# Decay factors from spread rows and a minimum, and local scores whose low key part meets half the rows

## The chip, the cores and the metric

The kernel runs on one core of a Trainium2 chip. The metric is the device time of one execution in microseconds (us). Before the change three runs gave 1501.08, 1501.22 and 1502.55 us; their median is 1501.22 us.

## The reference

The kernel computes one layer of an encoder trunk over 1024 tokens of width 1024: a mixer that joins windowed attention with a gated delta rule run in both directions, then a cross-attention into 256 memory tokens, then a SwiGLU FFN. The change touches two places in the mixer. In the windowed attention, 8 query heads of width 64 share 2 key heads, and a block of 128 queries sees itself and its two neighbour blocks:

```python
kw, vw = band(k), band(v)
scores = jnp.einsum('bnqhgd,bnkhd->bnhgqk', qb, kw) * (ATTN_HEAD_DIM ** -0.5)
```

In the delta rule, each chunk has a triangular matrix of decays, the exponent of a difference of running sums of g:

```python
g = jnp.cumsum(g.reshape(b, h, n, c), axis=-1)
decay = jnp.exp(jnp.where(incl, g[..., :, None] - g[..., None, :], -jnp.inf))
```

The rule runs once forward and once on the flipped sequence, with a g of its own for each direction.

## The kernel before

The mixer works in chunks of 128 tokens, so there are 8 chunks (`NT`). The product of a weight column block with all tokens (`proj`, L279) is 48 matmuls on TensorE of 512 columns each, because each operand is split in a rounded high part and a low rest (`split`, L100) and three of the four part products are kept.

A list written by hand, `ORDER_1` (L37), names the steps of the first stage: the projections `q`, `k`, `v` of four heads with a short convolution (`conv`, L291), and between them `E` (`decays`), `K` (`turned_keys`), `U` (`key_products`), `C` (`query_products`) and `B` (`base_inverse`). A scheduler then lays each engine's instructions in an order of its own from that program, so a step can stand far from where the list has it; every engine and each DMA queue runs its list in order. Nearly all DMAs are on SyncE's queue (SP).

`decays(h)` (L479) makes the two tiles `E` for head h, each of 4 chunks. Forward and backward decays stand in one tile, on the two sides of the diagonal. Four matmuls (two directions, and the high and the low part of g) of a triangular 0/1 matrix (`mL_r`, `mU_r`) with `gm`, the g of a chunk spread over the other triangular matrix, add up in one PSUM bank; `E` is the exponent of that. VectorE makes `gm` for heads 0 and 1 (L488), ScalarE for heads 2 and 3 (L491). `E` multiplies the key products `U` (L513) and the query products `pc` (L521).

The PSUM tiles of this stage come from a pool of five banks (`small`, L204). The tile that the change adds for the spread rows is taken from pool `ra`, whose two buffers of tag `rr` the attention projections use later.

`window(n, g)` (L663) does the local attention of query block n and key head g, 16 times. The keys `khi`, `klo` hold the 64 key channels twice, in rows 0 to 63 and in rows 64 to 127. `qs` holds the rounded queries in rows 0 to 63 and their low rest in rows 64 to 127 (a ScalarE cast at L676, then GpSimd on the lower half at L677); one matmul with `khi` over 128 rows so adds high times high and low times high. For each of four heads there are two matmuls, with `khi` and with `klo` (L685), of 384 columns, or 256 at the ends of the sequence; VectorE takes the scores out of PSUM with the band and the row's maximum (L687). The scores' banks come from pool `pw` with two buffers, shared with the transposes `ptw` of the weights. The windows run in between the projections of the second stage (`ORDER_2`) and the scan of the delta rule (`scan`, L830, matmuls L844) and the memory projections (`pck`, L984).

Of the kernel before, what the change touches and what calls it, by code (L numbers as in the profile page):

```python
# [19 lines left out]
P = 128  # L20
# [3 lines left out]
NT = S // P  # L24
HALF = 512
# [51 lines left out]
def tile_hybrid_block(  # L77
# [6 lines left out]
    nc = tc.nc  # L84
# [57 lines left out]
    mU_r = sm.tile([P, P], F32R, name="mU_r")  # L142
    mL_r = sm.tile([P, P], F32R, name="mL_r")
# [44 lines left out]

    d_beta = [dram.tile([32, P], F32, name=f"d_beta{g}") for g in range(2)]
# [14 lines left out]
    def small():  # L204
        return ps.tile([P, 512], F32, tag="ps", name="ps")
# [54 lines left out]
    with tc.issue_after(scaled.ins):  # L260
        nc.vector.tensor_copy(mU_r, cm["mU"])
        nc.vector.tensor_copy(mL_r, cm["mL"])

# [109 lines left out]
    ghi = sm.tile([P, 2, 4, NT], F32, name="ghi")  # L373
    glo = sm.tile([P, 2, 4, NT], F32, name="glo")
    ghr = t1.tile([P, 2, 4, NT], F32R, tag="ghr", name="ghr")
    nc.vector.tensor_copy(ghr, G)
    nc.vector.tensor_copy(ghi, f32(ghr))
    nc.vector.tensor_tensor(glo, G, ghi, ALU.subtract)

# [99 lines left out]
    def decays(h):  # L479

        for b in range(2):
            pa = small()
            n = 0
            for d, (mi, ml) in enumerate((("mUi", mL_r), ("mLi", mU_r))):
                for part in (ghi, glo):
                    gm = t2.tile([P, 4, P], F32R, tag="gm", name="gm")
                    if h < 2:
                        nc.vector.tensor_tensor(gm, bc(part[:, d, h, 4 * b:4 * b + 4], 2, (P, 4, P)), bc(cm[mi], 1, (P, 4, P)),  # L488
                                                ALU.mult)
                    for j in range(4 if h > 1 else 0):  # L490
                        nc.scalar.activation(gm[:, j, :], cm[mi], AF.Identity, scale=part[:, d, h, 4 * b + j:4 * b + j + 1])  # L491
                    nc.tensor.matmul(pa, ml, gm.rearrange("p c n -> p (c n)"), start=(n == 0), stop=(n == 3))
# [170 lines left out]
    def window(n, g):  # L663
# [13 lines left out]
        nc.gpsimd.tensor_tensor(qs[64:128], qr[64:128], f32(qs[64:128]), ALU.subtract)  # L677

# [3 lines left out]
        for hh in range(4):  # L682
            pp = pw.tile([P, 512], F32, tag="pw", name="psw")
            for i, kk in enumerate((khi, klo)):
                nc.tensor.matmul(pp[:, 0:w], qs[:, hh, :], kk, start=(i == 0), stop=(i == 1))  # L685
# [1209 lines left out]
```

## Time and profile before

| what | value |
|---|---|
| median of three runs | 1501.22 us |
| span of the profiled execution | 1497.9 us |
| time around the span, against the median | 3.3 us |
| mean granted TensorE clock | 0.995 |
| busy PE, weight load, VectorE, ScalarE, GpSimd | 98%, 83%, 74%, 52%, 25% of the span |
| DMA | 256.35 MB, 171 GB/s mean |

The profiled execution shows its span, from the first to the last instruction; its own time with what lies around the span is not listed beside it, so the three runs give it: about 3.3 us more than the span. A matmul's time in the trace runs from its start to a modelled end, and matmuls overlap in the array, so PE looks busy nearly always; how fast PE works is read from the distance between two starts. PEld is the load of the stationary operand, and a form such as 32*128 beside an operation gives the rows and columns of the array that it uses.

### The profile page before, as it was taken

The page shows a single profiled execution, that of the slowest core. Times are in us where ns is not written, and L with a number is a line of the kernel's source. Part 1 is how long each engine was busy: PE and PEld are TensorE (multiplying, and loading weights), DVE is VectorE, ACT ScalarE, POOL GpSimd, SP SyncE. Part 2 cuts the span into 40 slices and gives each one's busy share as a digit, 9 for nine tenths or more (in the row PEclk, how much of TensorE's full clock was granted, in tenths as well). Part 3 has the DMA queues.
Part 4 walks back from the last instruction along what each step waited for, and adds up shares of the span by engine and source line. Part 5 has one row for each costly group of instructions (what it writes and reads, how often), then busy time and mean ns, then how long its engine had stood idle before and what let it go on. Part 6 is the DMA issues. An engine that isn't in the chain of part 4 may idle for free.

```text
span 1497.9 us, 21340 instructions
## 1 busy us (share of the span) xinstructions
PE 1467.6 (98%) x7437; PEld 1239.1 (83%) x7437; DVE 1108.8 (74%) x1804; ACT 776.3 (52%) x1600; POOL 374.3 (25%) x411
## 2 busy tenths in 40 slices
PE   7999999999999999999999999999999999999998
PEld 6888878888999878888888877888888888888787
DVE  5878998577897866538767887686867774795666
ACT  7678844568567664555554774323223232544533
POOL 0011232442246213342201002343433342000030
PEclk9999999999999999999999999999999999999999
DMA  6244554657996585444855553343533433953355
GB/s 205 71 120 137 142 168 135 168 173 222 297 305 211 158 310 204 163 146 157 277 174 194 183 197 119 121 141 105 168 123 113 138 109 103 351 183 99 105 181 170
DMA packets 254169, 256.35 MB, mean 171 GB/s; under 512 B 18129, under 2 KB 186222, under 8 KB 254062
## 3 DMA queue, kind: packets, MB, share of 16 engines
q1 hardware_dynamic: 252141, 250.80, 52.7%
q0 software_dynamic: 768, 2.10, 0.5%
q10 hardware_dynamic: 1152, 2.10, 0.4%
q8 instruction: 58, 0.95, 0.3%
q14 instruction: 50, 0.40, 0.1%
HBM read 178.63 MB, written 73.70 MB: 168 GB/s over the span
## 4 chain that ended last, share of the span: by engine, by line
PE 73%; DVE 9%; ACT 4%; issue 2%; DMA 2%; SPq 1%; POOL 0%; DVEq 0%; ACTq 0%
PE pE L1511 8%; PE pD L1511 8%; PE pA L1511 6%; PE pmg L1105 6%; PE pcq L276 6%; PE pdX L1733 6%; PE pst L1324 5%; PE pdA L1733 4%; PE pB L1511 4%; PE pg L276 3%; PE psc L844 3%; PE pdD L1733 2%; PE pdX L1842 2%; PE pcs L1195 2%; PE pco L1222 1%
## 5 line engine op out<-in xcount | busy, mean ns | idle before, releaser
L103 ACT CAST whi<-wraw 128x1024 fp32r<-128x1024 f32 x96 | 100.7, 1050 | 119.5 <-DMA wraw<-in_w_gate_up_dram 40.0
L276 PE MATMUL pg<-hlo,whi 128*128 128x512 f32 x352 | 140.5, 399 | 0.0
L276 PE MATMUL pg<-hhi,whi 128*128 128x512 f32 x352 | 139.6, 396 | 0.0
L276 PE MATMUL pg<-hhi,wlo 128*128 128x512 f32 x352 | 139.2, 395 | 0.0
L104 POOL TENSOR_TENSOR wlo<-wraw,whi 128x1024 fp32r<-128x1024 f32 x37 | 90.3, 2440 | 191.1 <-ACT whi L103 179.1
L1511 PE MATMUL pA<-b,whi 128*128 128x512 f32 x352 | 109.7, 393 | 1.9 <-ACT whi L103 1.0
L104 DVE TENSOR_TENSOR wlo<-wraw,whi 128x1024 fp32r<-128x1024 f32 x59 | 72.5, 1228 | 31.1 <-ACT whi L103 27.0
L1511 PEld LDWEIGHTS pA<-b,whi 128*128 128x128 f32 x352 | 65.3, 188 | 17.1 <-ACT whi L103 1.9
L276 PEld LDWEIGHTS pg<-hhi,whi 128*128 128x128 f32 x352 | 66.6, 189 | 13.5 <-ACT hhi L241 0.3
L276 PEld LDWEIGHTS pg<-hlo,whi 128*128 128x128 f32 x352 | 66.8, 190 | 12.6
L276 PEld LDWEIGHTS pg<-hhi,wlo 128*128 128x128 f32 x352 | 66.8, 190 | 12.4
L1733 PE MATMUL pdX<-dhl,whi 128*128 128x512 f32 x264 | 76.1, 390 | 0.9 <-ACT dhl L103 0.7
L1603 POOL TENSOR_TENSOR act<-act,up 128x512 f32<-128x512 f32 x33 | 50.3, 1524 | 88.6 <-DVE up L1602 67.3
L103 ACT CAST whi<-araw 128x1024 fp32r<-128x1024 f32 (+1 forms) x36 | 35.3, 981 | 68.2 <-PE pdX L1733 27.6
L1511 PE MATMUL pA<-b,wlo 128*128 128x512 f32 x176 | 69.0, 392 | 0.5 <-DVE wlo L104 0.5
L104 DVE TENSOR_TENSOR wlo<-araw,whi 128x1024 fp32r<-128x1024 f32 (+1 forms) x36 | 40.8, 1132 | 33.6 <-ACT whi L103 33.5
L1574 POOL TENSOR_TENSOR sr<-wraw 128x512 f32<-128x512 f32 x22 | 30.0, 1363 | 139.1 <-DMA wraw<-in_w_gate_up_dram 87.1
L301 DVE SCALAR_TENSOR_TENSOR acc<-cp,cols,acc 128x1024 f32<-128x1024 f32 x48 | 63.1, 1316 | 0.2
L1733 PEld LDWEIGHTS pdX<-dhl,whi 128*128 128x128 f32 x264 | 49.3, 188 | 12.1 <-ACT dhl L103 1.1
L103 ACT CAST dhl<-b 128x512 fp32r<-128x512 f32 x66 | 40.3, 620 | 31.3 <-PE pdA L1733 13.5
L1575 DVE TENSOR_TENSOR sr<-sr,wraw 128x512 f32<-128x512 f32 x22 | 36.7, 1666 | 26.2 <-POOL sr L1574 26.2
L103 ACT CAST s0h<-sr 128x512 fp32r<-128x512 f32 x22 | 13.7, 622 | 79.1 <-POOL sr L1574 78.8
(504 smaller groups left out, 4331.5 us busy)
## 6 DMA issues: line engine op xcount, KB each, us to landing
wraw<-in_w_gate_up_dram SPq DMA_DIRECT2D x54, 512.0 KB, 3.9
kv<-d_kv SPq DMA_DIRECT2D x32, 512.0 KB, 6.0
wraw<-in_w_in_dram SPq DMA_DIRECT2D x22, 512.0 KB, 4.1
b<-in_w_down_dram SPq DMA_DIRECT2D x20, 512.0 KB, 6.3
araw<-d_as SPq DMA_DIRECT2D x20, 512.0 KB, 3.6
pz<-d_pz SPq DMA_DIRECT2D x32, 256.0 KB, 6.3
wraw<-in_w_ckv_dram SPq DMA_DIRECT2D x16, 512.0 KB, 5.0
wraw<-in_w_out_dram SPq DMA_DIRECT2D x16, 512.0 KB, 5.4
```

The source lines that it names most:

```text
L103: nc.scalar.copy(hi, src)
L104: return (eng or nc.vector).tensor_tensor(lo, src, f32(hi), ALU.subtract)
L276: nc.tensor.matmul(p_, w[:, k, :], ah[a][:, k, :], start=(k == 0 and i == 0), stop=(k == nk - 1 and i == 2))
L301: nc.vector.scalar_tensor_tensor(acc, cp[:, t:t + S], taps[t], acc, ALU.mult, ALU.add)
L844: nc.tensor.matmul(out[:, d, h, :], lt[:, d, h, :], rt[:, d, h, :], start=True, stop=True)
L1105: nc.tensor.matmul(pp[t], act[a][:, k, tt], w_[:, kk, :], start=(k == 0 and i == 0), stop=(k == KT - 1 and i == 2))
L1324: nc.tensor.matmul(bank, a[:, tt], w, start=(start and i == 0), stop=(stop and i == 2), skip_group_check=not check)
L1511: nc.tensor.matmul(out_, w[a][:, k, :], xx[b_][:, k, :], start=(start and k == 0 and i == 0), stop=(k == HK - 1 and i == 2), skip_group_ch ...
L1574: nc.gpsimd.tensor_tensor(s[0], b_[:, 0:HK], b_[:, HK:], ALU.add)
L1575: nc.vector.tensor_tensor(s[1], s[0], a_[:, 0:HK], ALU.subtract)
L1603: nc.gpsimd.tensor_tensor(o_, o_, up, ALU.mult)
L1733: nc.tensor.matmul(banks[t], a[:, k - k0, tt], w, start=(first and k == 0 and i == 0), stop=(k == NB - 1 and i == 2), skip_group_check=not ...
```

## The change

`decays` no longer uses TensorE. The running sums of g, which TensorE already made for another use (three small matmuls for each direction, the first of which gives the sums inside a chunk), are copied to `sums`, turned by one transpose, and written to a DRAM tile `d_sum`, one row for each direction, head and chunk. For each head and half, two DMAs read 512 sums and spread them over all 128 partitions (`ahead`). The difference between a spread sum and the partition's own sum is positive on the wrong side of the diagonal and not positive on the right one, for each direction on its own side, so the smaller of the two differences is the wanted exponent everywhere. ScalarE subtracts for the backward direction (four activations with a bias), VectorE subtracts for the forward one and takes the minimum, and ScalarE takes the exponent. The casts `mU_r`, `mL_r`, the split of G and the `gm` tiles go.

In `window`, the product with `klo` uses the high part of the queries alone. For the even head of a pair it takes rows 0 to 63; for the odd head a new tile `qo` holds the rounded queries in rows 64 to 127, and the matmul takes those rows. The two `klo` matmuls of a pair are written one behind the other, ahead of the two with `khi`, into two banks.

```diff
+    sums = sm.tile([P, 2, 4, NT], F32, name="sums")
+    nc.vector.tensor_copy(sums, pv[:, 0])
+    nsums = sm.tile([P, 4, NT], F32, name="nsums")
+    nc.vector.tensor_scalar(nsums, sums[:, 1], -1.0, None, ALU.mult)
...
+    pt = small()
+    nc.tensor.transpose(pt[0:64, 0:P], sums.rearrange("p d h c -> p (d h c)"), ident)
+    sT = t1.tile([64, P], F32, tag="sT", name="sT")
+    nc.vector.tensor_copy(sT, pt[0:64, 0:P])
+    nc.sync.dma_start(d_sum, sT)
...
     def decays(h):
 
+        by_row = d_sum.rearrange("(d h c) n -> d h (c n)", d=2, h=4)
         for b in range(2):
-            pa = small()
-            n = 0
-            for d, (mi, ml) in enumerate((("mUi", mL_r), ("mLi", mU_r))):
-                for part in (ghi, glo):
-                    gm = t2.tile([P, 4, P], F32R, tag="gm", name="gm")
-                    if h < 2:
-                        nc.vector.tensor_tensor(gm, bc(part[:, d, h, 4 * b:4 * b + 4], 2, (P, 4, P)), bc(cm[mi], 1, (P, 4, P)),
-                                                ALU.mult)
-                    for j in range(4 if h > 1 else 0):
-                        nc.scalar.activation(gm[:, j, :], cm[mi], AF.Identity, scale=part[:, d, h, 4 * b + j:4 * b + j + 1])
-                    nc.tensor.matmul(pa, ml, gm.rearrange("p c n -> p (c n)"), start=(n == 0), stop=(n == 3))
-                    n += 1
+            c4 = slice(4 * b, 4 * b + 4)
+            ahead = ra.tile([P, 2, HALF], F32, tag="rr", name="ahead", bufs=2)
+            for d in range(2):
+                nc.sync.dma_start(ahead[:, d], by_row[d, h, b * HALF:(b + 1) * HALF].partition_broadcast(P))
+            ahead = ahead.rearrange("p d (c n) -> p d c n", c=4)
             E = Es[h, b] = t2.tile([P, 4, P], F32, tag="E", name="E", bufs=4)
-            nc.scalar.activation(E, pa.rearrange("p (c n) -> p c n", c=4), AF.Exp)
+            for j in range(4):
+                nc.scalar.activation(ahead[:, 1, j], ahead[:, 1, j], AF.Identity, bias=nsums[:, h, 4 * b + j:4 * b + j + 1])
+            nc.vector.tensor_tensor(E, ahead[:, 0], bc(sums[:, 0, h, c4], 2, (P, 4, P)), ALU.subtract)
+            nc.vector.tensor_tensor(E, E, ahead[:, 1], ALU.min)
+            nc.scalar.activation(E, E, AF.Exp)
...
         nc.gpsimd.tensor_tensor(qs[64:128], qr[64:128], f32(qs[64:128]), ALU.subtract)
+        qo = tw.tile([P, 2, P], F32R, tag="qo", name="qo", bufs=1)
+        nc.scalar.copy(qo[64:128], qr[64:128, 1:4:2])
...
         for hh in range(4):
-            pp = pw.tile([P, 512], F32, tag="pw", name="psw")
-            for i, kk in enumerate((khi, klo)):
-                nc.tensor.matmul(pp[:, 0:w], qs[:, hh, :], kk, start=(i == 0), stop=(i == 1))
+            if hh % 2 == 0:
+                both = [pw.tile([P, 512], F32, tag="pw", name="psw") for _ in range(2)]
+                nc.tensor.matmul(both[0][:, 0:w], qs[0:64, hh, :], klo[0:64], start=True, stop=False)
+                nc.tensor.matmul(both[1][:, 0:w], qo[64:128, hh // 2, :], klo[64:128], start=True, stop=False)
+            pp = both[hh % 2]
+            nc.tensor.matmul(pp[:, 0:w], qs[:, hh, :], khi, start=False, stop=True)
```

The scheduler also lays the instructions anew. On TensorE, at the second window, the program before had these rows (`psw` are the scores, `pg` a projection, `ps<-ident,Ul` transposes of another step):

```order
L276 MATMUL pg<-hhi_152,wlo 128x512
L685 MATMUL psw<-khi,qs 128x384
L685 MATMUL psw<-klo,qs 128x384
L685 MATMUL psw<-khi,qs 128x384
L623 MATMUL ps<-ident,Ul 128x128 x4
L685 MATMUL psw<-klo,qs 128x384
```

The changed program has these at the same place, for the same two heads:

```order
L271 MATMUL pg<-hhi_151,whi 128x512
L683 MATMUL psw<-klo,qs 128x384
L686 MATMUL psw<-khi,qs 128x384
L271 MATMUL pg<-hlo_152,whi 128x512
L619 MATMUL ps<-ident,Ul 128x128 x4
L684 MATMUL psw<-klo,qo 128x384
L686 MATMUL psw<-khi,qs 128x384
```

The two matmuls with half the rows, `klo,qs` and `klo,qo`, no longer stand one behind the other. In all 16 windows there are 32 such pairs; two of them (the first pair of the first window and the first pair of the third) are neighbours on TensorE, and in the other 30 a matmul over 128 rows stands between them.

On SyncE's DMA queue, in the first stage where head 0's decays are made, the program before had these rows (`kt` turned keys, `acc` a convolution's result, `wraw` the weights of a coming projection):

```order
L756 DMA d_kv_103<-acc 128x8x128
L125 DMA wraw<-in_w_in_dram 128x8x128
L504 DMA d_kv_103<-kt 128x4x128 x2
L514 DMA d_u_109<-U 128x4x128 x2
L125 DMA wraw<-in_w_in_dram 128x8x128
```

The changed program has these there:

```order
L389 DMA d_sum<-sT 64x128
L500 DMA d_kv_101<-kt 128x4x128
L484 DMA ahead<-d_sum 128x512 x4
L500 DMA d_kv_101<-kt 128x4x128
L125 DMA wraw<-in_w_in_dram 128x8x128
L500 DMA d_kv_101<-kt 128x4x128
L484 DMA ahead<-d_sum 128x512 x2
```

The write of the sums and the four spreading reads for head 0 stand ahead of the next weight load, and head 1's reads follow it.

More of the change, by code (lines that the diff above doesn't have):

```diff
@@ L141, in tile_hybrid_block @@
     C = sm.tile([P, C1 - C0], F32, name="C")
-    mU_r = sm.tile([P, P], F32R, name="mU_r")
-    mL_r = sm.tile([P, P], F32R, name="mL_r")
     prm = sm.tile([P, 24], F32, name="prm")
@@ L187, in tile_hybrid_block @@
     d_u = [dram.tile([2, NT, P, P], F32, name=f"d_u{g}") for g in range(2)]
+    d_sum = dram.tile([2 * 4 * NT, P], F32, name="d_sum")
     d_beta = [dram.tile([32, P], F32, name=f"d_beta{g}") for g in range(2)]
@@ L259, in tile_hybrid_block @@
     nc.sync.dma_start(C, consts[:, C0:C1])
-    with tc.issue_after(scaled.ins):
-        nc.vector.tensor_copy(mU_r, cm["mU"])
-        nc.vector.tensor_copy(mL_r, cm["mL"])
     nc.sync.dma_start(prm[:, 0:8], a_log[0].rearrange("d h -> (d h)").partition_broadcast(P))
@@ L371, in tile_hybrid_block @@
     dump("beta", beta)
[L373 to L378, printed above, removed]
     pt = small()
```

## The prediction

> **What bounds the kernel now.** I read the page's totals first, then the busy time by stage, then TensorE's instructions in order of time, and last the chain of waits.
>
> ```profile
> span 1497.9 us, 21340 instructions
> PE 1467.6 (98%) x7437; PEld 1239.1 (83%) x7437; DVE 1108.8 (74%) x1804; ACT 776.3 (52%) x1600; POOL 374.3 (25%) x411
> PE 73%; DVE 9%; ACT 4%; issue 2%; DMA 2%; SPq 1%; POOL 0%; DVEq 0%; ACTq 0%
> 60.00:211.00 151.00, 151.00 (x783) 128.41 (x782) 130.00 (x198) 111.04 (x300) 23.18 (x43) 1.00 0.45 126
> 280.00:360.00 80.00, 78.99 (x462) 68.28 (x462) 52.62 (x132) 55.37 (x128) 29.31 (x63) 1.00 0.55 165
> 360.00:530.00 170.00, 163.12 (x1186) 151.27 (x1185) 145.87 (x363) 109.16 (x287) 68.74 (x82) 0.99 0.81 251
> ```
>
> The last three rows are stages: span of the stage, then PE, PEld, DVE, ACT and POOL busy, the clock, the DMA share. The decays lie in the first (60 to 211 us): PE is busy in all 151 us, DVE in 130. The windows lie in the other two. From 280 to 360 PE lacks 1.0 us, from 360 to 530 it lacks 6.9. So PE is the bound, tightly up to 360 us and loosely behind. PE's share of the chain over the whole span is 73%.
>
> A busy PE hides how long an instruction keeps the next one off. That is read from starts:
>
> ```profile
> 147.06 0.39 PE L276 MATMUL pg<-hlo,whi 128*128 128x512 f32 x1
> 147.28 0.39 PE L492 MATMUL ps<-gm,mL_r 128*128 128x512 f32 x1
> 147.51 0.39 PE L276 MATMUL pg<-hhi,wlo 128*128 128x512 f32 x1
> 341.34 0.42 PE L685 MATMUL psw<-khi,qs 128*128 128x384 f32 x1
> 341.60 0.34 PE L685 MATMUL psw<-klo,qs 128*128 128x384 f32 x1
> 341.77 0.34 PE L685 MATMUL psw<-khi,qs 128*128 128x384 f32 x1
> 341.95 0.33 PE L685 MATMUL psw<-klo,qs 128*128 128x384 f32 x1
> 342.12 0.39 PE L276 MATMUL pg<-hhi,wlo 128*128 128x512 f32 x1
> ```
>
> A 512-column matmul lasts 0.39 us but its successor starts 0.227 us later (147.28 to 147.51); one of 384 columns takes 0.17 us of PE's time (341.60 to 341.77). The first behind a group of unsplit 128-column products takes 0.26 (341.34 to 341.60), 0.09 more.
>
> **The decays, PE.** These rows are the instructions that go:
>
> ```profile
> L492 PE MATMUL ps<-gm,mL_r x16: 389/391/476, 70.2 to 159.3; 128*128 128x512 f32 x16
> L492 PE MATMUL ps<-gm,mU_r x16: 389/389/477, 76.1 to 165.4; 128*128 128x512 f32 x16
> L491 ACT ACTIVATE gm<-C,ghi x32: 385/392/495, 108.4 to 161.6; 128x128 fp32r<-128x128 f32 x32
> L491 ACT ACTIVATE gm<-C,glo x32: 384/391/414, 113.8 to 164.5; 128x128 fp32r<-128x128 f32 x32
> L488 DVE TENSOR_TENSOR gm<-ghi,C x8: 683/684/692, 67.3 to 105.7; 128x512 fp32r<-128x512 f32 x8
> L488 DVE TENSOR_TENSOR gm<-glo,C x8: 627/686/693, 69.6 to 107.5; 128x512 fp32r<-128x512 f32 x8
> L524 DVE TENSOR_TENSOR pm<-pc,C 128x512 f32<-128x512 f32 x16 | 10.6, 684 | 2.4 <-DMA d_pz<-pm 2.3
> ```
>
> PE loses 32 matmuls x 0.227 = 7.3 us, not the 12.5 us that 32 x 0.39 would say, and gains one transpose, 0.1 us. On VectorE, 16 `gm` products of 0.685 us go, and 16 come: a subtraction and a minimum for each of 8 half heads, both operands in SBUF as in `pm` (0.684), so the balance is nothing. The small casts and copies trade one for one. ScalarE loses 64 x 0.39 = 25 us, all of heads 2 and 3, and gains 32 activations of the same shape, 12.5 us; the exponent stays, now from SBUF.
>
> How much of the 7.3 us reaches the end? ScalarE gets lighter, and nothing of VectorE's is added, but VectorE then has its 130 us of work in about 144 instead of 151, in a fixed order with waits. The bounds are 0 (VectorE sets the pace at once) and 7.3. I take four fifths, 5.8 us: 130 in 144 is 90%, nearer to hidden than not.
>
> **The decays, the way round through DRAM.** Head 0's tile now waits for a copy, a transpose, a copy, a small write, spreading reads, then ScalarE and VectorE. Nearest rows:
>
> ```profile
> 68.69 0.48 PE L276 MATMUL pg<-hlo,whi 128*128 128x512 f32 x1
> 85.29 0.68 DVE L513 TENSOR_TENSOR U<-ps,E 128x512 f32<-128x512 f32 x1
> d_beta<-bT SPq DMA_DIRECT2D x2, 16.0 KB, 2.0
> d_u<-U SPq DMA_DIRECT2D x8, 256.0 KB, 2.3
> Ul<-d_u SPq DMA_DIRECT2D x8, 256.0 KB, 4.8
> L301 DVE SCALAR_TENSOR_TENSOR acc<-cp,cols,acc 128x1024 f32<-128x1024 f32 x48 | 63.1, 1316 | 0.2
> gpost<-in_g_ffn_post_dram SPq DMA_DIRECT2D x1, 512.0 KB, 9.6
> ```
>
> The first row is the end of the small matmuls that make the sums. In the new order the transpose stands 22 matmuls behind it (68.7 + 5.0 = 73.7), with the copies about 74.2; the write lands in 2.0 us, the four reads of 256 KB in 2.3 to 4.8 us (the one spread read with a landing, 512 KB, took 9.6), so they are there between 78.5 and 81; with about 5 us of arithmetic between other work, `U` comes near 86, against 85.3 before. PE reaches the second product of head 1, which needs a bank whose reader on ScalarE stands behind the last of these reads, near 84. So a wait of 0 to 4 us is possible; I take 1.0, since the readings of 256 KB end before that. Behind a late read wait, on VectorE, a convolution's steps (1.3 us each, L301), and on SP the next weight load. That load has cover: its weights are used a whole projection later (48 x 0.227 = 10.9 us). Later heads' reads start a step ahead and I cost them at nothing; if that cover fails it is the third rival.
>
> **The windows.** The number of matmuls (128) and their columns stay, so PE's streaming time does not fall unless two `klo` halves run side by side. Only 2 of 32 pairs are neighbours in the new order: 0.17 + 0.11 (a 256-column pair) = 0.3 us at best. Against it stands what happens where the used rows of the array change. The trace has one place, with transposes that use 32 rows:
>
> ```profile
> 53.94 0.39 PE L276 MATMUL pg<-hlo,whi 128*128 128x512 f32 x1
> 54.16 0.39 PE L276 MATMUL pg<-hhi,wlo 128*128 128x512 f32 x1
> 54.48 0.43 PE L339 MATMUL ps<-ident,abT 32*128 32x32 f32 x4
> 54.85 0.50 PE L276 MATMUL pg<-hhi,whi 128*128 128x512 f32 x1
> 55.19 0.40 PE L276 MATMUL pg<-hlo,whi 128*128 128x512 f32 x1
> L685 PE MATMUL psw<-khi,qs x64: 278/338/447, 280.1 to 529.3; 128*128 128x384 f32 x48, 128*128 128x256 f32 x16
> 54.48 0.32 PEld L339 LDWEIGHTS ps<-ident,abT 32*128 32x128 f32 x4 [0.35 <-ACT acc L302]
> 54.84 0.19 PEld L276 LDWEIGHTS pg<-hhi,whi 128*128 128x128 f32 x1
> 54.95 0.19 PEld L276 LDWEIGHTS pg<-hlo,whi 128*128 128x128 f32 x1
> ```
>
> Elsewhere the next weights load while a matmul streams (54.95 for the matmul at 55.19). Here both loads start with their own matmul (54.48, 54.84): nothing was prefetched across the change. Going in costs 54.48 - 54.16 - 0.227 = 0.09 us, coming out 55.19 - 54.85 - 0.227 = 0.11 us. The Trainium skill, TensorEngine Tiling (Key Properties), speaks against the change: a change of tiling mode drains the engine. The trace agrees, with 0.09 and 0.11 us.
>
> The new order has 62 islands of half rows (60 single, 2 double), each followed by a 128-row matmul. Coming out costs 62 x 0.11 = 6.8 us. Going in costs 0.09 us only where the row before isn't a 128-column product (behind such a one the 0.09 is paid already): 42 x 0.09 = 3.8 us. Together 10.6 us of PE. Of the islands 18 lie in the tight stretch up to 360 us, 29%, and count in full; the other 71% count with PE's share of the chain, 73%. So 10.6 x (0.29 + 0.71 x 0.73) = 8.6 us. Lower bound 0: 64 rows could behave unlike 32. Upper bound: a change waits for the whole pipeline, a matmul's length less its step, 0.338 - 0.170 = 0.168 us, twice for each island: 20.8 us, or 16.8 us at the end. I take 8.6, from the one place that shows it.
>
> ScalarE gets 16 copies `qo`, each half as wide as this cast or less:
>
> ```profile
> L676 ACT CAST qs<-qr 128x512 fp32r<-128x512 f32 x16 | 10.0, 622 | 22.4 <-DMA qr<-d_q 19.5 <-PE psw L685 2.9
> ```
>
> That is at most 16 x 0.62 = 10 us in 250 us in which it is busy for 165. But `qr` has one buffer and is free for the next window's load only after `qo`, some ScalarE steps later than GpSimd's reading before; ScalarE already waits 19.5 us for `qr`. Bounds 0 and 4 us (a quarter of a microsecond per window); I take 0.5, as the windows run ahead of their use.
>
> **The sum.** 1497.9 - 5.8 + 0.1 + 1.0 + 8.6 - 0.3 + 0.5 = 1502.0 us of span; with the 3.3 us between span and median, 1505.3 us. A measurement of this kernel can tell about 0.2%, 3 us, from no change: 1498.2 to 1504.2.
>
> **Rivals.** First, faster: the row change costs nothing for 64 rows, or the windows' slack hides it. For it speaks that PE lacks 6.9 us between 360 and 530; against it that it lacks only 1.0 up to 360, and the pair of rows above. It decides when the islands cost under about 1 us at the end. Then -7.3 + 0.1 + 1.0 + 0 to 3 us: 1495 to 1498 us, say 1496. A form of it: halves that use different rows run side by side everywhere, 24 x 0.17 + 8 x 0.11 = 5.0 us less, 1491 us. The Trainium skill, TensorE: Matmul & The Clock Gate (Part 3), states that matmuls in different row groups overlap, and also that they stay in program order; no row here shows two in flight at once. In that order 30 of 32 pairs have a 128-row matmul between them, so I give this form little.
>
> Second, a full drain at each change: 16.8 in place of 8.6 us, 1513.5 us. For it speaks only that a load was not started ahead; against it the measured 0.09 and 0.11.
>
> Third, the reads of `ahead` come late for all heads and VectorE, in order, stands behind them; then the 5.8 us are gone and the first wait is some 2 us longer: 1505.3 + 5.8 + 1 = 1512 us. For it: `gpost` took 9.6 us, and VectorE is 86% busy there. Against: DMA share is 0.45 in that stage.
>
> **Chances.** Forecast 0.45, its own range 1500 to 1511; first rival 0.25 (0.03 of it the paired form); second 0.15; third 0.15. Of the forecast 0.17 lies under 1504.2. So faster 0.25, same 0.17, slower 0.58. The range 1494 to 1514 leaves out about a tenth on each side.
>
> **What would show it.** Right: no L492, PE's starts still 0.227 us apart from 60 to 200 us, that stage done 5 to 7 us earlier; in the windows a `klo` row with form 64*128 whose weight load starts with it, and a `khi` row behind it about 0.1 us long in the step; the end of the scan later than before by 2 to 6 us. Wrong: `khi` following `klo` after 0.17 us (first rival), after 0.34 us (second), or VectorE idle for `ahead` in many places (third). If the stage from 60 to 211 us gains nothing, the four fifths was the wrong step.

## The result, and the profile after

The changed kernel takes 1535.5 us (median of 4 runs, 1532.3 to 1542.4), the kernel before 1501.2 us beside it. The ratio is 1.0241, with a 95% interval of 1.0213 to 1.0269: slower by 34 us. The prediction said slower, but 1505.3 us, with a range that ended at 1514. The profiled execution of the changed kernel is the longest of its four (1542.4 us), so its trace shows some 7 us more than the median does. Its span is 1540.6 us, so some 1.8 us lie around a span and not 3.3: the other 1.5 us ahead of the prediction lie between the profiled execution of the kernel before and the median. The forecast was built on the median, so the difference that it forecast, 4.1 us, stands.

First the page of the changed kernel (span, busy time by engine):

```profile
span 1540.6 us, 21293 instructions
PE 1494.2 (97%) x7406; PEld 1242.0 (81%) x7406; DVE 1099.4 (71%) x1802; ACT 764.3 (50%) x1576; POOL 388.5 (25%) x411
```

TensorE has 31 instructions fewer (7406 against 7437) and is busy 26.6 us longer. It also stands idle 46 us instead of 30 (span less busy). Both need an explanation. The three stages of the prediction, from the busy times by stretch (stretch, its length, then PE, PEld, DVE, ACT and POOL, the clock, the DMA share):

```profile
60.00:211.00 151.00, 145.44 (x750) 123.02 (x749) 130.33 (x200) 96.46 (x264) 31.96 (x44) 0.99 0.58 155
280.00:360.00 80.00, 78.40 (x400) 63.88 (x398) 44.83 (x110) 44.93 (x109) 25.38 (x57) 0.91 0.43 126
360.00:530.00 170.00, 161.70 (x1111) 140.61 (x1110) 125.00 (x336) 104.33 (x278) 68.47 (x80) 0.98 0.78 238
```

In the decays' stage TensorE is no longer busy throughout: 5.6 of 151 us are idle. From 280 to 360 us it is as busy as before, but gets through 400 matmuls instead of 462, and its clock is 0.91 instead of 1.00. From 360 to 530 it gets through 1111 instead of 1186.

Where does this reach the end? The out projection (`pmg`) takes the scan's results (`psc`) and the windows' outputs (`pow`). The rows with `s0h` are its first half, tokens 0 to 511; it needs the end of the scan, but of the windows only those of its own tokens. The second half follows at once and needs the last window. These rows group the last matmuls of each, first of the kernel before, then of the changed one; the two numbers ahead of the semicolon are the first and the last start:

```profile
L844 PE MATMUL psc<-vn,pz x128: 270/275/275, 366.7 to 497.4; 128*128 128x128 f32 x128
L717 PE MATMUL pow<-pl,vhl x44: 389/403/504, 312.1 to 554.5; 128*128 128x512 f32 x44
L1105 PE MATMUL pmg<-whi,s0h x64: 389/389/792, 531.5 to 580.4; 128*128 128x512 f32 x64
L1105 PE MATMUL pmg<-wlo,s0h x64: 389/389/628, 533.8 to 580.8; 128*128 128x512 f32 x64
```

```profile
L845 PE MATMUL psc<-vn,pz x128: 270/275/422, 382.9 to 521.8; 128*128 128x128 f32 x128
L718 PE MATMUL pow<-pl,vhl x44: 392/474/796, 313.7 to 597.9; 128*128 128x512 f32 x44
L1106 PE MATMUL pmg<-whi,s0h x64: 389/389/793, 558.9 to 620.4; 128*128 128x512 f32 x64
L1106 PE MATMUL pmg<-wlo,s0h x64: 387/389/483, 561.9 to 620.8; 128*128 128x512 f32 x64
```

The scan ends 24.4 us later, the last window 43.4 us later, and the first half of the out projection 40.0 us later. Behind it nothing more is lost but 2.7 us (the spans differ by 42.7). So nearly the whole loss is made before 621 us, in two places. The out projection starts 27.4 us later (558.9 against 531.5), 37 us behind the end of the scan, where it was 34 before. And its first half takes 12.6 us more (61.9 against 49.3): TensorE's order has the matmuls of the last windows in between, and there are more of them left (243 matmuls in all against 217), with 4.4 us idle and a clock of 0.92 against 0.97. In each of the 18 kernels with a trace the start stands 33 to 37 us behind the end of the scan.

### The profile page after: what moved, and what is told of

It is laid out like the page before. It is cut to its first block, busy times and chain, and to the rows that moved or that the text cites. A ratio compares the mean times of both kernels' runs of the same rounds, so it can differ in the third digit from the quotient of the medians.

```text
span 1540.6 us, 21293 instructions
## 1 busy us (share of the span) xinstructions
PE 1494.2 (97%) x7406; PEld 1242.0 (81%) x7406; DVE 1099.4 (71%) x1802; ACT 764.3 (50%) x1576; POOL 388.5 (25%) x411
## 4 chain that ended last, share of the span: by engine, by line
PE 71%; DVE 10%; DMA 5%; issue 2%; ACT 2%; SPq 1%; POOL 0%; DVEq 0%; ACTq 0%; POOLq 0%
PE pE L1512 7%; PE pD L1512 7%; PE pcq L271 6%; PE pdX L1734 6%; PE pmg L1106 5%; PE pA L1512 5%; PE pst L1325 5%; PE pg L271 5%; PE psc L845 3%; PE pB L1512 3%; PE pdA L1734 2%; PE pdD L1734 2%; PE pdX L1843 2%; PE pcs L1196 1%; PE pck L985 1%
## 5 line engine op out<-in xcount | busy, mean ns | idle before, releaser
L104 DVE TENSOR_TENSOR wlo<-araw,whi 128x1024 fp32r<-128x1024 f32 (+1 forms) x36 | 40.9, 1135 | 34.4 <-ACT whi L103 34.3
L1575 POOL TENSOR_TENSOR sr<-wraw 128x512 f32<-128x512 f32 x22 | 30.3, 1375 | 136.5 <-DMA wraw<-in_w_gate_up_dram 86.3
L688 DVE CUSTOM_DVE_ANT_0 sc<-psw,C,prm 128x384 f32<-128x384 f32 (+1 forms) x64 | 37.1, 581 | 34.4 <-PE psw L686 33.8
L1734 PEld LDWEIGHTS pdX<-dhl,whi 128*128 128x128 f32 x264 | 49.3, 188 | 12.1 <-ACT dhl L103 1.1
```

What stands on the lines that cost most here:

```text
L104: return (eng or nc.vector).tensor_tensor(lo, src, f32(hi), ALU.subtract)
L1734: nc.tensor.matmul(banks[t], a[:, k - k0, tt], w, start=(first and k == 0 and i == 0), stop=(k == NB - 1 and i == 2), skip_group_check=not ...
```

## The experiments

Each run has its own runs of the kernel before beside it. The number given is the difference of the medians, and the ratio with its 95% interval. Nearly every edit makes the scheduler lay the instructions of the middle stages anew, so that a difference can come from the new order as well as from the edit. Two comparisons, both of half rows with full rows, keep the order of every engine, and are pointed out.

### The two parts apart

**Decays alone**: the function `window` of the kernel before in the changed kernel.

> Only the decays are changed, the windows are those of before. Theory A (each change of rows in the windows drains TensorE and is the loss): the profile of the changed kernel is 1.2 us behind at the end of the first stage, with one wait of 3.15 us and a halved clock right behind it in that; so about 1502 us, 1498 to 1505. Theory B (the copies qo, the one buffer qr and the two banks taken at once hold the windows up): the same here, 1498 to 1505. Theory C (the late reads of ahead are the loss): 1520 us or more.

Measured: 1508.8 us, 9.5 more than before, 1.0069 (1.0044 to 1.0093). **Windows alone**: the `window` of the changed kernel in the kernel before.

```
-    mU_r = sm.tile([P, P], F32R, name="mU_r")     (mL_r likewise)
+    mU_r = tb.tile([P, P], F32R, tag="mU_r", name="mU_r", bufs=1)
```

> Only the windows are changed, the decays are those of before (two constant tiles are moved to another pool, to make room for qo). Theories A and B: nearly the whole loss, 1530 to 1545 us. Theory C: 1501 to 1510 us.

Measured: 1529.3 us, 30.0 more, 1.0213 (1.0192 to 1.0235). The windows make most of the loss, as theories A and B had it (0.7 us under their range). But the decays lose more than was read from the trace, where I had expected nearly nothing: 1508.8 us lies in no theory's range. The two parts add up to 39.5 us, 5 more than both together cost, so they are not independent of each other.

### Half rows against full rows, in the same order

```
-        nc.scalar.copy(qo[64:128], qr[64:128, 1:4:2])
+        nc.scalar.copy(qo, qr[:, 1:4:2])
-                nc.tensor.matmul(both[0][:, 0:w], qs[0:64, hh, :], klo[0:64], start=True, stop=False)
-                nc.tensor.matmul(both[1][:, 0:w], qo[64:128, hh // 2, :], klo[64:128], start=True, stop=False)
+                nc.tensor.matmul(both[0][:, 0:w], qs[:, hh, :], klo, start=True, stop=False)
+                nc.tensor.matmul(both[1][:, 0:w], qo[:, hh // 2, :], klo, start=True, stop=False)
```

> The changed kernel, but both klo products run over 128 rows (qo is copied over 128 rows; for odd heads the low part meets the high part of the queries twice instead of high and low). The order of instructions, the two banks at once, qo and its waits stay. Theory A: the klo step is 0.17 us again instead of 0.37, and the time falls to that of the decays alone, 1498 to 1508 us. Theory B: the time stays at 1528 us or more. Theory C: it stays at 1528 us or more.

Measured: 1523.4 us, 24.0 more than before, 1.0169 (1.0147 to 1.0190). So about 10 us of the 34 (ratios 1.0241 and 1.0169; their half widths together are 0.36%, 5 us) belong to the half rows. The time lies in no theory's range, and theory A alone falls: 14 us remain over the decays alone with no half row in the program. The order of every engine is the same in both, so the two traces can be laid side by side. The third window's first pair, in order of time, first with half rows, then with full rows:

```profile
315.98 0.40 PE L718 MATMUL pow<-pl,vhl 128*128 128x512 f32 x1
316.31 0.44 PE L683 MATMUL psw<-klo,qs 64*128 64x384 f32 x1
316.31 0.44 PE L684 MATMUL psw<-klo,qo 64*128 64x384 f32 x1
316.68 0.62 PE L686 MATMUL psw<-khi,qs 128*128 128x384 f32 x2
317.14 0.40 PE L271 MATMUL pg<-hhi,whi 128*128 128x512 f32 x1
```

```profile
310.44 0.39 PE L718 MATMUL pow<-pl,vhl 128*128 128x512 f32 x1
310.67 0.34 PE L683 MATMUL psw<-klo,qs 128*128 128x384 f32 x1
310.85 0.34 PE L684 MATMUL psw<-klo,qo 128*128 128x384 f32 x1
311.02 0.51 PE L686 MATMUL psw<-khi,qs 128*128 128x384 f32 x2
311.37 0.39 PE L271 MATMUL pg<-hhi,whi 128*128 128x512 f32 x1
```

This is one of the two neighbouring pairs. Its halves start at the same time: they do run side by side. But going in takes 0.33 us instead of 0.23, the step out 0.37 instead of 0.17, and the two `khi` behind it 0.46 instead of 0.35. From `pow` to `pg` it is 1.16 us against 0.93: even where the overlap works, the half rows lose 0.23 us a pair. Where the halves stand alone, each pays by itself (changed kernel, the same window's second pair, matmuls and then the load of the first `khi`):

```profile
321.05 0.44 PE L683 MATMUL psw<-klo,qs 64*128 64x384 f32 x1
321.42 0.44 PE L686 MATMUL psw<-khi,qs 128*128 128x384 f32 x1
321.78 0.44 PE L684 MATMUL psw<-klo,qo 64*128 64x384 f32 x1
322.15 0.45 PE L686 MATMUL psw<-khi,qs 128*128 128x384 f32 x1
322.44 0.40 PE L271 MATMUL pg<-hhi,whi 128*128 128x512 f32 x1
```

```profile
321.41 0.19 PEld L686 LDWEIGHTS psw<-khi,qs 128*128 128x128 f32 x1 [0.18 <-issue]
```

`klo` to `khi` takes 0.37 us (321.05 to 321.42), and `khi` to the next 0.29 behind it (322.15 to 322.44), where full rows take 0.17 each. The load of `khi`'s weights (last row) starts with its own matmul, not ahead of it. With the 0.10 for going in, a single stretch of half rows costs 0.10 + 0.20 + 0.11 = 0.41 us, 62 of them 25 us of TensorE. The busy time grows by about as much, 1494.2 us against 1468.6 with full rows, 25.6 more, though the first trace is the longest of its four executions and the second the shortest. The time grows by about 10 of these 25.

### The copies qo

**One bank at a time**, half rows as in the change:

```
+            pp = pw.tile([P, 512], F32, tag="pw", name="psw")
             if hh % 2 == 0:
-                both = [pw.tile([P, 512], F32, tag="pw", name="psw") for _ in range(2)]
...
-            pp = both[hh % 2]
```

> The changed kernel, half rows and qo kept, but each head takes its bank when its turn comes, as before (klo half, then khi, head after head; no two banks at once). Two theories for the 14 us by which the changed windows with full rows (1523 us) are slower than the decays alone (1509 us). B1 (a pair holds both banks that the turned scores also need): the time falls by those 14 us, to 1518 to 1525. B2 (qo has one buffer, and qr waits for it, so the next window is loaded late): no change, 1530 to 1538 us.

Measured: 1533.1 us, 32.9 more, 1.0219 (1.0204 to 1.0234). **The same with full rows:**

> The same with full rows: one bank at a time, klo over 128 rows, qo copied over 128 rows and used for odd heads (the low part meets the high part twice there). B1: the time of the decays alone, 1506 to 1512 us. B2: as with both banks at once, 1519 to 1526 us.

Measured: 1522.9 us, 22.7 more, 1.0158 (1.0133 to 1.0182). Both stay where they were with two banks at once. B1 falls: that a pair holds both banks is not the 14 us. These two kernels also have the same order on every engine, so they measure the half rows a second time: 10.2 us, and again 0.37 us against 0.175 from `klo` to `khi` (medians). TensorE's busy time grows by 16.4 us here (1485.8 against 1469.4) at clocks of 0.993 and 0.989, so the 25 us above is good to some 9.

**Without qo:**

```
-        nc.gpsimd.tensor_tensor(qs[64:128], qr[64:128], f32(qs[64:128]), ALU.subtract)
-        qo = tw.tile([P, 2, P], F32R, tag="qo", name="qo", bufs=1)
-        nc.scalar.copy(qo[64:128], qr[64:128, 1:4:2])
+        for o, r in enumerate((slice(64, 128), slice(0, 64))):
+            nc.gpsimd.tensor_tensor(qs[r, o:4:2], qr[r, o:4:2], f32(qs[r, o:4:2]), ALU.subtract)
...
-                nc.tensor.matmul(both[1][:, 0:w], qo[64:128, hh // 2, :], klo[64:128], start=True, stop=False)
+                nc.tensor.matmul(both[1][:, 0:w], qs[64:128, hh + 1, :], klo[64:128], start=True, stop=False)
```

> The changed kernel without qo: odd heads keep the high part of their queries in the upper row half of qs itself and the low part in the lower, so two smaller GpSimd subtractions replace one and a copy on ScalarE goes; both banks at once and half rows stay. B1: no change, 1530 to 1538 us. B2: 14 us less, 1518 to 1525.

Measured: 1520.6 us, 20.4 more, 1.0141 (1.0120 to 1.0161): 14 us less than the changed kernel, as B2 said. **Two buffers for qo:**

```
-        qo = tw.tile([P, 2, P], F32R, tag="qo", name="qo", bufs=1)
+        qo = tw.tile([P, 2, P], F32R, tag="qo", name="qo", bufs=2)
```

> The changed kernel with two buffers for qo in place of one (an unused kilobyte per partition at the end of vhl makes room). If the one buffer is what costs (the next window's qo waits for the matmuls of the window before, its qr is not released, and the load of the queries behind it on SP's queue waits): as without qo, 1518 to 1525 us. If it is the copy itself on ScalarE, or that qr is released by ScalarE instead of GpSimd: no change, 1530 to 1538.

Measured: 1524.0 us, 23.7 more, 1.0162 (1.0139 to 1.0184): the copy stays and 11 of the 14 us go, so most of it is the single buffer. Both this edit and the one without `qo` lay the middle stages anew, so a part of their gain may be the order; that the two agree, and that one bank at a time, which moves about as many of TensorE's rows, changed only 2 us, speaks against it. The waits between 270 and 640 us (engine and line, what it waited for, sum, times, longest), of the changed kernel and then with two buffers:

```profile
ACT qo L675 <- PE psw L684: 17.2, 8, 4.2
SPq L670 <- ACT qo L675: 29.8, 6, 22.7
```

```profile
ACT qo L675 <- PE psw L684: 13.8, 8, 4.5
SPq L670 <- POOL qs L673: 24.3, 3, 20.3
SPq L670 <- ACT qo L675: 1.1, 1, 1.1
```

The sums do not show the gain. With two buffers ScalarE still waits 13.8 us for the matmuls of a window before, and the load of the queries (L670) on SP's queue waits for GpSimd's split in place of `qo`. What differs is how far the load runs ahead. These rows are the last window's queries, first of the changed kernel (the copy `qo` of the window before, the load, the cast), then with two buffers, then of the kernel before (load and cast):

```profile
532.97 0.41 ACT L675 CAST qo<-qr 64x256 fp32r<-64x256 f32 x1
533.44 1.25 SPq L670 DMA_DIRECT2D qr<-d_q  x2
539.01 0.61 ACT L672 CAST qs<-qr 128x512 fp32r<-128x512 f32 x1
```

```profile
500.93 1.24 SPq L670 DMA_DIRECT2D qr<-d_q  x2
516.45 0.62 ACT L672 CAST qs<-qr 128x512 fp32r<-128x512 f32 x1
```

```profile
479.08 2.29 SPq L674 DMA_DIRECT2D qr<-d_q  x2
494.35 0.64 ACT L676 CAST qs<-qr 128x512 fp32r<-128x512 f32 x1
```

In the changed kernel the load can't start until `qo` of the window before has read `qr`, and that `qo` can't start until the window before it has used the one buffer (its last `klo,qo` matmul starts at 532.03). So the load starts 5.6 us ahead of the cast. With two buffers it starts 15.5 us ahead, as in the kernel before (15.3 us). How the shorter lead turns into 11 us was not followed further. The trace with two buffers is of the longest of its five executions (1531.6 us).

### All pairs side by side

Both `khi` come first, and the two `klo` halves directly behind them and behind one another: 32 stretches, all 32 pairs neighbours.

```
+                for i in range(2):
+                    high = nc.tensor.matmul(both[i][:, 0:w], qs[:, hh + i, :], khi, start=True, stop=False)
+                with tc.issue_after(high.ins), tc.high_priority(3 * AHEAD):
+                    nc.tensor.matmul(both[0][:, 0:w], qs[0:64, hh, :], klo[0:64], start=False, stop=True)
+                    nc.tensor.matmul(both[1][:, 0:w], qo[64:128, hh // 2, :], klo[64:128], start=False, stop=True)
```

> The changed kernel, but khi of both heads is issued first and the two klo halves directly behind one another: 32 stretches of half rows instead of 62, and all 32 pairs side by side. Theory A: a stretch costs about 0.20 us leaving it, 0.11 behind that and 0.1 entering, so 62 x 0.41 = 25 us fall to 13, and 30 pairs that overlap save some 5 us: about 1518 us, 1508 to 1524, unless stalls keep halving the clock. Theory B: no change, 1530 us or more. Theory C: no change.

Measured: 1542.4 us, 43.0 more, 1.0290 (1.0264 to 1.0316). The same without `qo`:

> Without qo (1520.6 us), and with khi of both heads first and the two klo halves directly behind one another: 32 stretches of half rows, all pairs side by side. If the rest of the windows' loss (12 us over the decays alone) is the change of rows: half the stretches cost 6 us, and the pairs that overlap take back up to 5, so 1509 to 1516 us. If it is the two banks held at once or the order of the products: 1519 us or more.

Measured: 1529.5 us, 29.2 more, 1.0201 (1.0181 to 1.0221). The range for fewer stretches is missed in both, and on the wrong side: 7 and 9 us slower than with 62 stretches, although TensorE has less to do (1478.5 us busy against 1484.0, both without `qo`). The second time lies in the range for the banks or the order of the products. The rows of this last kernel say where it went:

```profile
L846 PE MATMUL psc<-vn,pz x128: 272/275/377, 374.9 to 495.2; 128*128 128x128 f32 x128
L719 PE MATMUL pow<-pl,vhl x44: 387/477/796, 311.3 to 586.2; 128*128 128x512 f32 x44
L1107 PE MATMUL pmg<-wlo,s0h x64: 388/389/628, 548.7 to 608.9; 128*128 128x512 f32 x64
```

The scan ends at 495.2, earlier than in the kernel before (497.4). The last window ends at 586.2, 31.7 us later, and the out projection 28.1 us later. The out projection starts at 532.1, within a microsecond of the kernel before, but its first half takes 76.8 us instead of 49.3, with late windows in it. Against the kernel without `qo`, the scan ends 17.5 us earlier and the last window 15.0 later. Why the windows lag in this order is not settled; what is shown is that less work on TensorE did not bring the end forward.

### The decays and their late reads

**Reads that are there from the start:**

```
-                nc.sync.dma_start(ahead[:, d], by_row[d, h, b * HALF:(b + 1) * HALF].partition_broadcast(P))
+                nc.sync.dma_start(ahead[:, d], x[4 * d + h, b * HALF:(b + 1) * HALF].partition_broadcast(P))
...
-            nc.scalar.activation(E, E, AF.Exp)
+            nc.scalar.activation(E, E, AF.Exp, scale=0.001)
```

> Only the decays are changed (windows as before), and the spread rows are read from the input x, which is there from the start, in place of the sums (so the decays are other numbers, and their exponent is scaled by 0.001 to keep them finite); the sums are still turned and written. If the late reads are what costs (first product with the decays 5 us later, one wait of 3.15 us of TensorE, a halved clock behind it): that wait goes, and the time falls from 1509 to between 1494 and 1501 us. If it is the added work of ScalarE and VectorE that costs: 1505 us or more.

Measured: 1501.5 us, 1.3 more, 1.0017 (1.0001 to 1.0032), against 1508.8 for the decays alone, 7 us less and 0.5 above the range for the late reads. But the edit does less than its name. Only head 0's reads come ahead (issued from 20.3 us). Those of head 1 are issued from 76.2 us instead of 87.5, as the two buffers come free earlier, and ScalarE stands 8.1 us for reads all the same (8.2 with the decays alone). What goes is TensorE's one wait of 3.2 us, and the first `U` comes at 81.3 instead of 90.3 us. The stages are laid anew as well, so the 7 us are what earlier reads and the new order are worth together. In the changed kernel the waits of the stage from 60 to 211 us, the DMA row of the reads and the group of `U`, the first product with the decays, read:

```profile
ACT ahead L488 <- DMA ahead<-d_sum: 7.6, 3, 4.2
PE ps L457 <- DVE U L509: 3.1, 1, 3.1
```

```profile
ahead<-d_sum SPq DMA_DIRECT2D x16, 256.0 KB, 4.9
```

```profile
L509 DVE TENSOR_TENSOR U<-ps,E x8: 630/684/692, 91.5 to 168.8; 128x512 f32<-128x512 f32 x8
```

The first `U` comes at 91.5 instead of 85.3 us. The first read is issued at 79.3 us, a read lands 4.9 us after its issue (median; I had taken 2.3 to 4.8), and head 1's reads are issued only from 88.6, when head 0 releases the two buffers. TensorE stands once for 3.1 us, near 101 us.

But with earlier reads nothing is won either. The last projection matmul of that kernel, and its scan, windows and out projection:

```profile
L271 PE MATMUL pg<-hhi,wlo x352: 387/389/628, 16.4 to 350.2; 128*128 128x512 f32 x176
L840 PE MATMUL psc<-vn,pz x128: 272/275/317, 362.6 to 496.2; 128*128 128x128 f32 x128
L713 PE MATMUL pow<-pl,vhl x44: 389/475/628, 306.8 to 554.5; 128*128 128x512 f32 x44
L1101 PE MATMUL pmg<-wlo,s0h x64: 387/389/628, 533.1 to 580.8; 128*128 128x512 f32 x64
```

Before, the last such projection matmul started at 356.1: it is 5.9 us earlier, almost exactly the 5.8 that I had counted for TensorE. The scan gives it back to 1.2 us, and window and out projection end at 554.5 and 580.8 as before (to the tenth by chance: executions of the kernel before differ by up to 9 us).

**Earlier reads of the true sums**: the sums are turned in the bank where they stand, and copy, turn, write and reads have precedence.

```
+    with tc.high_priority(AHEAD):
+        nc.tensor.transpose(pt[0:64, 256:384], sums.rearrange("p d h c -> p (d h c)"), ident)
...
+            with tc.high_priority(AHEAD):
+                ahead = ra.tile([P, 2, HALF], F32, tag="rr", name="ahead", bufs=2)
```

> Only the decays changed, windows as before. The sums are turned in the bank in which they stand, and their copy, turn, write and the spread reads have precedence, so the turn stands about four matmuls earlier and the reads of head 1 follow those of head 0 on SP's queue. If lateness of the reads is the loss of the decays (1508.8 against 1501.5 us with reads that are there from the start): the wait near 100 us shortens, and the time falls to between, 1501 to 1507 us. If it is not: 1507 to 1512 us.

Measured: 1508.0 us, 7.6 more, 1.0053 (1.0037 to 1.0070). That is in the range for lateness not being the loss. But the first reads did not come earlier on the chip (issued from 79.3 us, against 78.2 with the decays alone), and TensorE's wait near 100 us grew to 4.8 us, so this says nothing on lateness. It says something else: the scan ends at 491.4 us, 6.0 earlier than before, but the windows at 564.2, 9.7 later, and the out projection at 587.6, 6.8 later.

**Heads 2 and 3 alone by spread rows**, heads 0 and 1 by matmuls: `decays(h)` calls the new form `if h > 1`, else the old one.

> The decays of heads 0 and 1 by matmuls as before, those of heads 2 and 3 by spread rows and a minimum, whose reads then have several projections of time; the windows of before. 16 of the 32 matmuls and 64 x 0.39 us of ScalarE go. If the late reads of the first two heads are the loss of the decays: no wait of 3 us near 100 us, and the time falls to that with the reads ready from the start (1501.5) or below it, 1494 to 1501 us. If not: 1505 us or more.

Measured: 1521.6 us, 21.2 more, 1.0162 (1.0135 to 1.0188): the side on which late reads are not the loss. The windows end at 576.0 and the out projection at 601.7. With half of the change, and the half that should be free, it loses twice as much as with all of it. Its trace has a wait for late reads all the same (60 to 211 us):

```profile
ACT ahead L501 <- DMA ahead<-d_sum: 10.0, 2, 5.7
```

The scheduler put head 2's reads so early in ScalarE's order that ScalarE stands 5.7 us for the first of them, up to 86.3 us. TensorE waits 3.3 us for a `gm` product of VectorE at 95.9, and the first `U` comes at 97.5, 12 us later than in the kernel before. So this kernel does not free the first heads from late reads. That the decays lose 9.5 us is measured; how much of it is the late reads and how much the new order stays open.

### Precedence for the windows

All of a window's instructions get precedence of 400 places in the scheduler (150 in the last of the four).

```
-                next(wins[-1])
+                with tc.high_priority(400):
+                    next(wins[-1])
...
-                next(last, None)
+                with tc.high_priority(400):
+                    next(last, None)
```

> The changed kernel, and every window's instructions are given precedence over the others by the scheduler (400 places), so that the windows run ahead of the scan instead of behind it. Theory L (the loss reaches the end because the windows finish late: the out projection needs the last one, and in every run so far it ends 23 to 28 us behind the last window's output): the last window's scores stand before the end of the values' projection, and the time falls by 8 to 20 us, to 1515 to 1528. Rival M (the loss is TensorE's own time in drains and in waits, wherever the windows stand): 1532 to 1540 us.

Measured: 1528.7 us, 27.9 more than before, 1.0180 (1.0150 to 1.0211): 6.5 us less than the changed kernel, short of the 8 to 20 of theory L, but under rival M's range.

> The kernel before with the same precedence for its windows. Theory L: the windows set the end there as well, so the time falls a little, 1492 to 1499 us, if the scan is not held up more. Rival M: the scan falls behind by what the windows gain, 1500 to 1512 us.

Measured: 1512.7 us, 11.9 more, 1.0083 (1.0056 to 1.0110): rival M's side.

> Only the decays changed (1508.8 us), with the same precedence for the windows of before. Theory L: less than 1508, 1496 to 1505 us. Rival M: 1507 to 1518 us.

Measured: 1511.6 us, 10.8 more, 1.0073 (1.0045 to 1.0101): no gain, rival M.

> The decays of heads 2 and 3 alone by spread rows (1521.6 us, whose windows ended 32 us later than before and whose out projection ended 21 us later), with precedence of 150 places for the windows. Theory L: the 21 us go for the most part, 1498 to 1510 us. Rival M (the loss stands in the first stages): 1515 us or more.

Measured: 1508.9 us, 8.1 more, 1.0064 (1.0043 to 1.0085): 13 us of the 21 come back, theory L.

So precedence helped in the two kernels whose windows lag far, and helped nothing or hurt in the two whose windows don't. The kernel before with windows first shows why:

```profile
L846 PE MATMUL psc<-vn,pz x128: 270/275/377, 384.1 to 512.7; 128*128 128x128 f32 x128
L717 PE MATMUL pow<-pl,vhl x44: 389/396/774, 302.7 to 553.9; 128*128 128x512 f32 x44
L1107 PE MATMUL pmg<-wlo,s0h x64: 388/389/501, 547.3 to 592.1; 128*128 128x512 f32 x64
```

The last window ends at 553.9, as before, but the scan at 512.7, 15.3 us later, and now the out projection starts late and ends 38 us behind the last window instead of 26. So two things set its end. The end of the scan sets its start, and what the windows have left to do inside it sets its length: its first half takes 46 us with the windows first, 49 in the kernel before, 62 in the changed one. What one gains the other can give back. None of the versions beats the kernel before.

## Why the prediction was right or wrong

The sign was right, but the loss is 34.4 us where 4.1 were forecast (1505.3 less 1501.2). In medians, the decays alone cost +9.5, where the prediction had them at -4.7 (-5.8 + 0.1 + 1.0). The half rows cost about +10.5 (34.4 less 24.0; without `qo` 20.4 less 9.5 is 10.9), where it had +8.3 (8.6 less 0.3). `qo` cost about +14 (34.4 less 20.4; 24.0 less 9.5 is 14.5), where it had +0.5. So two steps failed, by about 14 us each: the copies `qo` and the decays. The islands came out near their size, by luck, as two errors met.

**"I take 0.5, as the windows run ahead of their use."** It was reasoned from the busy time of ScalarE (165 of 250 us) and a bound of 4 us. A lead there was, in the loads: in the kernel before, the last window's load of queries starts 15.3 us ahead of its cast. The single buffer cut it to 5.6. I named the load of `qr` behind `qo`, but not that `qo` itself waits for the matmuls of the window before. And the windows' end has no lead over the start of the out projection: the last `pow` of the kernel before, at 554.5, stands behind it (531.5), among its matmuls, so that a late window makes it longer. Measured about 14 us instead of 0.5.

**The islands, 8.6 us at the end (10.6 of TensorE).** The mechanism was right: the load that is not started ahead, 0.09 expected and 0.10 measured going in, 0.11 and 0.11 behind the first 128-row matmul. The number of stretches was right too. (The row of the load at 54.48 also names a wait for ScalarE, so the 0.09 was not the change of rows alone for certain.) What was missing is the change itself: 0.20 us between the half-row matmul and the 128-row one. The one place of the trace had four small transposes ahead of the change, and the step from the last of them to the matmul was inside the 0.37 us from 54.48 to 54.85, which I did not take apart. Taken apart, it is 0.15 us, where the four stand 0.06 apart, so that place shows 0.09 of the 0.20. I also set going in to nothing behind a 128-column product; between the same-order kernels it costs 0.17 there (median). So 25 us of TensorE instead of 10.6, more than the 20.8 of my upper bound. The Trainium skill, TensorE: Matmul & The Clock Gate (Single matmul latency), puts the constant part of the latency of a single bf16 matmul, with its drain, at about 166 ns at full clock. Here the change took 0.20 us, with other operands; an estimate from that figure would have come near. That 81% of it should reach the end was wrong the other way: about 10 of 25 do. So 8.6 us came close to 10.5 although neither factor was right.

**The first stage.** TensorE's 7.3 us went as counted, ScalarE lost 14.6 us (111.04 to 96.46; 12.5 expected), VectorE stayed (130.0 and 130.3). "1.0 us, 0 to 4" for the way through DRAM was wrong. `U` was to come near 86 us and came at 91.5: the reads were issued at 79.3 where I had reckoned about 76, took 4.9 us, and head 1's waited for buffers, which I had costed at nothing. TensorE's wait of 3.1 us is within the 0 to 4, but the clock is 0.99 instead of 1.00 in that stage, and earlier reads with a new order saved 7 us. The third rival had the wait and its place, on head 1, but not its price: without its 8.8 us for the windows (8.6 - 0.3 + 0.5) its 1512 us are 1503, and the decays alone took 1508.8. And four fifths of the 7.3 reaching the end was wrong: 5.9 us reached the end of the projections with earlier reads, and none the end of the out projection. That freed time of TensorE gives nothing there is shown; which wait took it is not.

**What would show it.** `klo` with form 64*128 and its own late load: yes. `khi` about 0.1 us longer: yes, but behind a step of 0.37, which is the second rival's sign. The scan later by 2 to 6 us: it was 24. The second rival's 1513.5 us had the drain of TensorE nearer (20.8 us against 25) and the rest of the sum wrong.

**The clock**, which the prediction left at 0.995, fell to 0.988: (1 - 0.988) x 1540.6 = 18 us against 7.5. In the changed kernel, the matmul at 337 us, for which TensorE waited 1.21 us for VectorE, and the granted clock by stretch (PE busy, clock, DMA share, GB/s):

```profile
337.02 0.79 PE L718 MATMUL pow<-pl,vhl 128*128 128x512 f32 x1 [1.21 <-DVE pl L104]
```

```profile
336.00:338.00 2.00, 0.98 (x2) 0.62 0.43 162
338.00:350.00 12.00, 12.00 (x37) 0.50 0.01 4
350.00:354.00 4.00, 4.00 (x21) 0.98 0.23 73
```

Some 13 us at half clock follow a wait of 1.2 us, and cost about 6.5 us in a stage in which TensorE was the bound. No run separates the clock from the waits that it follows, so it is part of the three terms, not a fourth. The half rows' 10 us are not the clock's: with full rows it is 0.989.

## What to carry to other kernels

Before costing a stage at "hidden", look for the last instruction of each chain that the next stage needs, and how far the next stage's end stands behind it; here a scan that ended 2 to 6 us earlier gained nothing when the windows ended later. A copy that is small in busy time can hold back the next load when it has one buffer whose reader stands a step later. And matmuls over half the rows did not pay in runs of one or two: a pair that overlaps perfectly was still 0.23 us slower than two full-row matmuls of 384 columns among other work. Longer runs of them were not tried. Last, an edit that makes a scheduler lay the instructions anew tests the new order as well: precedence alone, with no other change, made the kernel before 12 us slower.

## What the runs showed of the hardware

- A change from 64 to 128 rows costs 0.2 us at the change (0.37 us instead of 0.17 for 384 columns, 0.31 instead of 0.12 for 256), then 0.11 in the next step, and 0.10 going in.
- Two matmuls in different row halves start in the same hundredth of a microsecond (316.31 and 316.31).
- A wait of 1.21 us, with one of 0.39 us shortly ahead of it, was followed by some 13 us at half clock, in which TensorE had hardly a gap. The Trainium skill, TensorE: Matmul & The Clock Gate (Why this matters for your kernels), warns of idle gaps over about 3 us; the trace shows the halving behind less.
- A spread read of 256 KB from one row of 2 KB landed in 4.9 us (median of 16).
